# Moving GpSimd's two-input elementwise operations to VectorE's queue in a two-layer decoder trunk

## The chip, the core and the metric

The kernel runs on one core of one Trainium2 chip. The metric is the device time of one execution in microseconds (us); the time before is the median of three runs. Below, PE is TensorE's matmul pipe, DVE is VectorE, ACT is ScalarE, POOL is GpSimd and SP is SyncE, whose queue issues every DMA of this kernel.

## The reference, cut to what matters

The input x is 512 tokens by 1024 features, in float32, and there are two layers. For each layer six modulation vectors come from one matrix product of silu(c) with ada_w.

```
h    = x * (1 + scale1) + shift1
proj = h @ w_in                      # 512 columns a, 512 u, 512 v
y_a  = trailing-window means of a (windows 2, 4, 8, 16) minus a, times pool_w, times pool_scale
y_b  = gelu(u) * (tril(W_s) @ layernorm(gelu(v)) + b), per head, in chunks of 128 tokens
x    = layernorm(alpha * x + gate1 * (concat(y_a, y_b) @ w_out))
h    = x * (1 + scale2) + shift2
g, val = split(h @ w_up)
x    = layernorm(alpha * x + gate2 * ((gelu(causal_conv3(g)) * val) @ w_down))
```

## The kernel before, in words

Each engine takes its instructions in the order in which the program writes them. PE computes every large product in three passes over float32r parts: weights and activations are each split into a high part (a rounded copy) and a low part (the value minus the high part), and the passes are high by high, high by low and low by high.

**Weights.** SP loads 512 KB blocks of 128 x 1024 into one of seven buffers `raw`. `wsplit_next` (L116) makes the high part `whi` on ACT (L132) and then the low part `wlo` with one two-input subtraction (L135). `refill(n, eng, defer)` (L153) does this for the next n weights and orders loads ahead; `eng` says which engine takes the subtraction, VectorE if nothing is given. A `raw` buffer is free again when its subtraction has been done, and the load that takes the buffer waits for that in SP's queue.

**Modulation sums.** `ada_sum` (L180) is one DVE operation of 128 x 1024 over a loaded `raw` block with an accumulated column. `first_h` (L458) runs two of them for each of the eight k-tiles of the first layer's h, and `pump` (L229) spreads the others between other work. These blocks share the seven `raw` buffers with the weights.

**Start.** For each k-tile SP loads two ada_w blocks, a tile of x and zero to two w_in blocks; `first_h` forms the scale and shift columns, the high part `hh` (DVE, L466), the exact value (ACT, L467) and the low part `hl` (L468, on DVE for the first two k-tiles and on POOL for the other six). PE takes each k-tile as it comes.

**Token mixing.** `window_sums(g, eng)` (L535) doubles windows by shifted adds (L540) and small copies (L541); `pool_group` (L547) finishes a group. `v_norm` (L571) normalizes v; `z_mix` (L584) and `pool_mix` (L558) make the eight inputs of the output projection and free their PSUM banks. In layer 0 all this stands between PE's u tiles, its z and pm products and the output projection (`project`, L340, with the products in L336 to L338).

**Norms.** `project_and_norm` (L353) computes the second half of a projection chunk by chunk (four chunks of 128 tokens), with `residual` (L287: a multiplication out of PSUM, L291, and an add into `xr`, L292), statistics, `rstd_of` (two tiny POOL operations, L274 and L275), the normalization (L383), transposes (L298) and `modulate` (L301), whose low part `hl` is L313. While the last chunk is under way up to three weights are prepared; the subtraction of the first stands before that chunk's residual, those of the others behind its statistics:

```
refill(4 - len(ready), G, lows)
...
mv, rs = rstd_of(sts[c], f"{tag}{c}")
for f in lows[1:]:
    f()
```

`next_residuals` (L316) runs eight POOL operations of 128 x 1024 behind a norm (L318, L319). `norm_rows` loads the rows g and b that they need, behind the weights in SP's queue, and ACT scales them (L327). `project_and_end` (L389) is the last norm.

Before the change POOL's queue takes these two-input operations, besides `next_residuals` and the tiny ones: the low parts of the first layer's w_in and w_out and of the weights prepared in a norm's last chunk, six of the eight `hl` of the start, the windows of pooling group 3 in layer 0, the adds of three first-half residuals in each of the three inner norms, and four such adds in the last one.

Of the kernel before, what the change touches and what calls it, by code (L numbers as in the profile page):

```python
# [38 lines left out]
def trunk(ctx: ExitStack, tc: tile.TileContext, a: dict, out: bass.AP):  # L39
# [10 lines left out]

    # each engine takes its instructions in the order they are written here
    ctx.enter_context(tc.manual_schedule())
# [14 lines left out]

    # ---- constants; 2 silu(c) along every partition
    c_in = const.tile([P, KD], F32, name="c_in")
# [25 lines left out]

    # ---- the weights in the order of their use: float32 in, two float32r parts out
    order = []
# [55 lines left out]
    def refill(n=1, eng=None, defer=None, in_units=False):  # L153
        """Prepares the next n weights, as far as there is room for them."""
        for _ in range(n):
            if count["split"] < len(order) and (in_units or count["live"] < N_SPLIT):
                wsplit_next(in_units, eng, defer)
                while count["load"] < min(len(order), count["split"] + count["ahead"]):
                    wload()
# [8 lines left out]
    def mm3(ps, w, x, start, stop):  # L168
        """ps += (wh + wl).T @ (xh + xl)"""
        T.matmul(ps, w[0], x[0], start=start, stop=False)  # L170
        T.matmul(ps, w[0], x[1], start=False, stop=False)  # L171
        T.matmul(ps, w[1], x[0], start=False, stop=stop)  # L172

    # ---- adaLN: columns of silu(c) @ ada_w, 128 at a step, that fill in between other work
    ada = [(0, v) for v in (2, 4, 3, 5)] + [(1, v) for v in (1, 0, 2, 4, 3, 5)]
# [17 lines left out]
    def gate_start(l, v):  # L193
        """The gate's columns on the diagonals of blocks, in two float32r parts."""
        g = modc[l][:, 8 * v : 8 * v + 8]
        gh = small.tile([P, KD], F32R, tag="gh", name=f"gh{l}_{v}")
        gl = small.tile([P, KD], F32R, tag="gl", name=f"gl{l}_{v}")
        V.tensor_copy(gh, g)
        V.tensor_tensor(gl, g, gh.bitcast(F32), op=ALU.subtract)
        out_ = []  # L200
        for hf in range(2):
            for part in (gh, gl):
                d = unit(f"gd{l}_{v}_{hf}", F32R)
                V.tensor_tensor(
                    d.rearrange("p (j n) -> p j n", j=4),
                    ident.unsqueeze(1).to_broadcast([P, 4, P]),
                    part[:, 4 * hf : 4 * hf + 4].bitcast(F32).unsqueeze(2).to_broadcast([P, 4, P]),
                    op=ALU.mult,
                )
                out_.append(d)  # L210
        return out_

    def ada_flush(now=False):
        """Gates along every partition: the diagonals two calls after the columns, the products
        two calls later."""
        for due in ada_due:
            due[0] += 1
            if due[3] is None and (now or due[0] >= 2):
                due[3] = gate_start(*due[1:3])
        while ada_due and (now or ada_due[0][0] >= 4):  # L220
            _, l, v, d = ada_due.pop(0)
            gates[l, v] = rows.tile([P, D], F32, tag="gate", name=f"gate{l}_{v}")
            for hf in range(2):
                ps = bank(f"gate{l}_{v}_{hf}")
                T.matmul(ps, ones_r, d[2 * hf], start=True, stop=False)
                T.matmul(ps, ones_r, d[2 * hf + 1], start=False, stop=True)
                A.copy(gates[l, v][:, halves(hf)], ps)

    def pump(n=1, upto=None):  # L229
        """n steps of the sums, as far as these are for the vectors upto."""  # L230
        for _ in range(n):
            i = ada_at["step"]
            if i >= len(ada) or (upto is not None and ada[i][:2] not in upto):
                return
            ada_load(max(0, min(i + 1 + ADA_AHEAD, len(ada)) - ada_at["load"]))
            l, v, n_ = ada[i]
            ada_sum(l, v, n_, ada_raw.pop(0))
            if n_ == KD - 1:
                o = slice(8 * v, 8 * v + 8)
                V.tensor_tensor(modc[l][:, o], modc[l][:, o], cols[l][:, C_ADAB + 8 * v : C_ADAB + 8 * v + 8], op=ALU.add)  # L240
                if v in (2, 5):
                    ada_due.append([0, l, v, None])
            ada_at["step"] += 1

    def weave(gens, side=()):
        """The steps of gens in turn, those of side in between."""
        gens, side = list(gens), list(side)
        while gens or side:
            gens = [g for g in gens if next(g, 0) is None]
            if side:  # L250
                side.pop(0)()

    def affine_cols(l, sub, g, b):
        """Columns A, B with h = n * A + B, from the last norm's g and b and the modulation."""
        o = 24 * sub
# [12 lines left out]

    # ---- post-norm: xr holds the sum; leaves n, h, and the next residual
    def rstd_of(st, name):  # L270
# [7 lines left out]
    def affine_norm(t, mv, rs, g, b, pieces=1, after=None):  # L278
        """t = (t - mean) * rstd * g + b"""
        V.scalar_tensor_tensor(t, t, mv[:, 0:1], g, op0=ALU.subtract, op1=ALU.mult)  # L280
# [6 lines left out]
    def residual(ps, c, hf, gate, eng=None, f=slice(0, HALF)):  # L287
        """Columns f of half hf."""
        t = unit(f"res{c}_{hf}")
# [4 lines left out]
    def turn(c, tag):  # L294
        """n of one chunk, transposed."""
        ps = [bank(f"tr_{tag}{c}_{hf}") for hf in range(2)]
# [4 lines left out]
    def modulate(c, ps, tag, AB):  # L301
        """h of one chunk from its transposed n, in two halves."""
        ca, cb = AB
# [26 lines left out]
    def pair_mms(ps, c, w, act, i, n, f=slice(0, HALF)):  # L330
        """A pair of k-tiles i, i + 1 of n, for columns f of one chunk."""
        cs = slice(c * P, (c + 1) * P)
# [7 lines left out]
    def project(act, hf, name, after):  # L340
        """All chunks at once against streamed weights; after(i) follows each pair."""
        ps = [bank(f"{name}{hf}_{c}") for c in range(NCH)]
# [10 lines left out]
    def project_and_norm(act, ps0, gate, tag, AB):  # L353
        """The second half chunk by chunk, each chunk's norm under the next one's products.
        ps0 holds the first half. Leaves the last chunk to be turned."""
        n = len(act)
# [4 lines left out]
        for c in range(NCH):  # L361
# [6 lines left out]
            if c == NCH - 1:  # L368
                refill(4 - len(ready), G, lows)
                for f in lows[:1]:  # L370
                    f()
# [14 lines left out]
            if c + 1 < NCH:  # L386
                residual(ps0[c + 1], c + 1, 0, gate, G)

    def project_and_end(act, ps0, gate, grow, brow):  # L389
        """The same at the end, where the norm goes out; the last chunk's columns in two parts."""  # L390
        n = len(act)
# [6 lines left out]
        def first_half(c):  # L398
            sts[c] = small.tile([P, 4, 6], F32, tag="st4", name=f"end{c}")
            residual(ps0[c], c, 0, gate, G)  # L400

# [30 lines left out]
    def after_norm(name, tag, AB):  # L432
        """The first four tiles after a norm: in halves of the tokens, the last chunk turned
        in the midst of the first half."""
        tiles = []
# [11 lines left out]

    # ---- start: modulation of the first layer and h from x, one k-tile after the other
    A0 = const.tile([P, KD], F32, name="A0_0")
# [8 lines left out]
    def first_h(k, x, raw):  # L458
# [8 lines left out]
        A.activation(x, x, AF.Identity, bias=B0[:, o], scale=A0[:, o])  # L467
        (V if k < 2 else G).tensor_tensor(hl[:, k, :], x, hh[:, k, :].bitcast(F32), op=ALU.subtract)  # L468

    def v_mms(ps, w, k):  # L470
        """k-tile k of all chunks of v, tokens on partitions."""
        wh, wl = w[0](4 * (k % 2), 4)
# [8 lines left out]
    for k in range(KD):  # L481
        at = first_load(k)
        new = FIRST[k]
        wload(len(new))
        refill(min(1, len(new)), G)
        first_h(k, *at)
        refill(len(new) - 1, G)
        fresh = []
# [16 lines left out]
    wload(3)  # L505
    refill(1, G)
    count["ahead"] = AHEAD
    done = [ps for ps, w in tiles]

    for l in range(L):  # L510
        col = cols[l]

        # ======== token mixing
        fill = () if l else ((0, 2), (0, 4), (0, 3))
# [95 lines left out]

        lo_eng = None if l else G
        if l:
# [10 lines left out]
        else:  # L623
            pump(PRE_FILL, fill)
            refill(1, G)
        w3 = wst.rearrange("p (h t) -> p h t", h=4)
# [11 lines left out]
        for i in range(4):  # L638
# [10 lines left out]
            if i == 0 and l == 0:  # L649
                window_sums(2, V)  # L650
                window_sums(3, G)
                pool_group(2)
# [22 lines left out]

        # ======== channel mixing
        more = l + 1 < L
# [122 lines left out]
```

## Time and profile before

| | |
|---|---|
| runs, us | 1043.29, 1040.75, 1042.89; median 1042.89 |
| profiled execution | span 1041.6 us, from its first to its last instruction; no other time of it is given |
| PE busy | 990.9 us (95%) |
| DVE busy | 695.7 us (67%) |
| ACT busy | 352.8 us (34%) |
| POOL busy | 214.0 us (21%), 136 instructions |
| mean granted TensorE clock | 0.980 |

The span is the time from the first to the last instruction of one profiled execution; it lies inside the range of the three runs, 1.3 us under their median. A busy share is an average over the whole span, and the stages of this kernel differ.

### The profile page before, as it was taken

The page shows a single profiled execution, that of the slowest core. Times are in us where ns is not written, and L with a number is a line of the kernel's source. Part 1 is how long each engine was busy: PE and PEld are TensorE (multiplying, and loading weights), DVE is VectorE, ACT ScalarE, POOL GpSimd, SP SyncE. Part 2 cuts the span into 40 slices and gives each one's busy share as a digit, 9 for nine tenths or more (in the row PEclk, how much of TensorE's full clock was granted, in tenths as well). Part 3 has the DMA queues.
Part 4 walks back from the last instruction along what each step waited for, and adds up shares of the span by engine and source line. Part 5 has one row for each costly group of instructions (what it writes and reads, how often), then busy time and mean ns, then how long its engine had stood idle before and what let it go on. Part 6 is the DMA issues. An engine that isn't in the chain of part 4 may idle for free.

```text
span 1041.6 us, 11987 instructions
## 1 busy us (share of the span) xinstructions
PE 990.9 (95%) x4654; PEld 826.8 (79%) x4654; DVE 695.7 (67%) x896; ACT 352.8 (34%) x495; POOL 214.0 (21%) x136
## 2 busy tenths in 40 slices
PE   5996889999999999999999999999999999999996
PEld 4785568888888888888888878888888888888886
DVE  6989998788673456757579973878744245444446
ACT  3242316443432123334254331644343212333210
POOL 4647245800000000000039300680000000000022
PEclk7998899999999999999999999999999999999999
DMA  9873772276574336547603422227433332334002
GB/s 334 306 276 110 287 279 76 90 259 211 194 228 135 102 101 200 183 147 257 203 21 114 160 81 81 83 94 250 141 101 101 101 101 81 101 101 142 21 1 81
DMA packets 44695, 154.57 MB, mean 148 GB/s; under 512 B 5216, under 2 KB 5472, under 8 KB 44640
## 3 DMA queue, kind: packets, MB, share of 16 engines
q1 hardware_dynamic: 44640, 153.82, 43.6%
q8 instruction: 36, 0.59, 0.2%
q14 instruction: 19, 0.16, 0.0%
HBM read 151.71 MB, written 2.10 MB: 148 GB/s over the span
## 4 chain that ended last, share of the span: by engine, by line
PE 82%; DVE 10%; POOL 3%; DMA 2%; issue 2%; ACT 1%; SPq 0%; DVEq 0%; POOLq 0%; ACTq 0%
PE up L171 15%; PE up L172 15%; PE up L170 15%; PE down L336 6%; PE down L338 6%; PE down L337 6%; PE n_pj L336 2%; PE n_pj L338 2%; PE n_pj L337 2%; DVE raw_ada L182 2%; POOL wlo L135 1%; DMA b<-in_ln_b_dram 1%; PE out L338 1%; PE v L475 1%; PE v L476 1%
## 5 line engine op out<-in xcount | busy, mean ns | idle before, releaser
L171 PE MATMUL up<-hl,whi 128*128 128x512 f32 (+1 forms) x768 | 285.6, 372 | 4.8 <-DVE hl L313 4.8
L172 PE MATMUL up<-hh,wlo 128*128 128x512 f32 (+1 forms) x768 | 285.4, 372 | 1.0 <-POOL wlo L135 1.0
L170 PE MATMUL up<-hh,whi 128*128 128x512 f32 (+1 forms) x768 | 285.5, 372 | 0.0
L135 DVE TENSOR_TENSOR wlo<-raw_w_up,whi 128x1024 fp32r<-128x1024 f32 x81 | 111.7, 1381 | 135.6 <-ACT whi L132 135.6
L171 PEld LDWEIGHTS up<-hl,whi 128*128 128x128 f32 x768 | 144.6, 188 | 30.5 <-DVE hl L313 5.6
L172 PEld LDWEIGHTS up<-hh,wlo 128*128 128x128 f32 x768 | 144.6, 188 | 26.4 <-POOL wlo L135 1.4
L170 PEld LDWEIGHTS up<-hh,whi 128*128 128x128 f32 x768 | 144.6, 188 | 24.9
L135 DVE TENSOR_TENSOR wlo<-raw_w_down,whi 128x1024 fp32r<-128x1024 f32 x44 | 53.9, 1225 | 114.0 <-ACT whi L132 114.0
L132 ACT CAST whi<-raw_w_up 128x1024 fp32r<-128x1024 f32 x88 | 91.0, 1045 | 69.1 <-PE down L338 52.6
L182 DVE SCALAR_TENSOR_TENSOR raw_ada<-raw_ada,c 128x1024 f32<-128x1024 f32 x80 | 106.4, 1341 | 4.1 <-DMA raw_ada<-in_ada_w_dram 4.1
L336 PE MATMUL down<-whi,gh 128*128 128x512 f32 x272 | 105.8, 389 | 0.0
L337 PE MATMUL down<-wlo,gh 128*128 128x512 f32 x272 | 105.8, 389 | 0.0
L338 PE MATMUL down<-whi,gl 128*128 128x512 f32 x272 | 105.8, 389 | 0.0
L274 POOL TENSOR_SCALAR rs_n<-mv_n 128x1 f32<-128x1 f32 x12 | 5.8, 485 | 397.5 <-DVE mv_n L272 397.5
L292 POOL TENSOR_TENSOR xr<-res,xr 128x512 f32<-128x512 f32 x13 | 16.6, 1289 | 321.8 <-DVE res L291 319.6
L694 ACT ACTIVATE y<-y 128x512 f32<-128x512 f32 x44 | 27.9, 634 | 148.8 <-DVE y L691 148.8
L132 ACT CAST whi<-raw_w_down 128x1024 fp32r<-128x1024 f32 x44 | 46.0, 1047 | 74.8 <-PE down L338 74.8
L684 ACT ACTIVATE y<-up,cols 128x512 f32<-128x512 f32 x44 | 34.3, 779 | 80.0 <-PE up L172 80.0
L338 PEld LDWEIGHTS down<-whi,gl 128*128 128x128 f32 x272 | 51.1, 188 | 10.6
L336 PEld LDWEIGHTS down<-whi,gh 128*128 128x128 f32 x272 | 51.1, 188 | 10.6
L337 PEld LDWEIGHTS down<-wlo,gh 128*128 128x128 f32 x272 | 51.1, 188 | 10.6
L310 ACT ACTIVATE ht_n<-tr_n,B,A 128x128 f32<-128x128 f32 x96 | 36.1, 455 | 57.2 <-PE tr_n L298 41.2
(155 smaller groups left out, 1620.7 us busy)
## 6 DMA issues: line engine op xcount, KB each, us to landing
raw_w_up<-in_w_up_dram SPq DMA_DIRECT2D x88, 512.0 KB, 3.3
raw_ada<-in_ada_w_dram SPq DMA_DIRECT2D x80, 512.0 KB, 4.2
raw_w_down<-in_w_down_dram SPq DMA_DIRECT2D x44, 512.0 KB, 3.3
raw_w_in<-in_w_in_dram SPq DMA_DIRECT2D x24, 512.0 KB, 4.3
raw_first<-in_ada_w_dram SPq DMA_DIRECT2D x16, 512.0 KB, 5.3
raw_w_out<-in_w_out_dram SPq DMA_DIRECT2D x16, 512.0 KB, 4.1
xT<-in_xT_dram SPq DMA_DIRECT2D x8, 256.0 KB, 5.4
xr<-in_x_dram SPq DMA_DIRECT2D x4, 512.0 KB, 6.5
```

The lines of the kernel that those rows point to most:

```text
L132: A.copy(hi, src)
L135: (eng or V).tensor_tensor(lo, src, hi.bitcast(F32), op=ALU.subtract)
L170: T.matmul(ps, w[0], x[0], start=start, stop=False)
L171: T.matmul(ps, w[0], x[1], start=False, stop=False)
L172: T.matmul(ps, w[1], x[0], start=False, stop=stop)
L182: V.scalar_tensor_tensor(raw, raw, 0.5, c2, op0=ALU.mult, op1=ALU.mult, accum_out=modc[l][:, o : o + 1])
L310: A.activation(tmp[:, w], ps[hf][:, w], AF.Identity, bias=cb[:, k : k + 1], scale=ca[:, k : k + 1])
L336: T.matmul(ps[:, f], ah[:, cs], wh, start=i + j == 0, stop=False)
L337: T.matmul(ps[:, f], ah[:, cs], wl, start=False, stop=False)
L338: T.matmul(ps[:, f], al[:, cs], wh, start=False, stop=i + j == n - 1)
L684: A.activation(y, pg, AF.Identity, bias=col[:, C_CB + j : C_CB + j + 1], scale=col[:, cw + 2 : cw + 3])
L694: A.activation(y, y, AF.Gelu_apprx_tanh)
```

## The change

Every `tensor_tensor` of POOL up to the norms' end goes to VectorE's queue, at the place in the program where it stood: `refill` is no longer given GpSimd, the first layer's `hl` are all on VectorE, so are the four windows of group 3 with their four small copies, and the first-half residual adds. `next_residuals`, `rstd_of` and the mask of the spatial weights stay on POOL. The other lines of the diff take comments away.

```diff
-                refill(4 - len(ready), G, lows)
+                refill(4 - len(ready), None, lows)
...
-                residual(ps0[c + 1], c + 1, 0, gate, G)
+                residual(ps0[c + 1], c + 1, 0, gate)
...
-            residual(ps0[c], c, 0, gate, G)
+            residual(ps0[c], c, 0, gate)
...
-        (V if k < 2 else G).tensor_tensor(hl[:, k, :], x, hh[:, k, :].bitcast(F32), op=ALU.subtract)
+        V.tensor_tensor(hl[:, k, :], x, hh[:, k, :].bitcast(F32), op=ALU.subtract)
...
-        refill(min(1, len(new)), G)
+        refill(min(1, len(new)))
         first_h(k, *at)
-        refill(len(new) - 1, G)
+        refill(len(new) - 1)
...
-    refill(1, G)
+    refill(1)
...
-        lo_eng = None if l else G
+        lo_eng = None
...
-            refill(1, G)
+            refill(1)
...
-                window_sums(3, G)
+                window_sums(3, V)
```

## Rows read from the trace of the kernel before

**Rows 1.** Busy time by stretch: length, engines' busy us, PE clock, DMA share, GB/s.

```profile
84.00:115.20 31.20, 17.85 (x67) 11.71 (x65) 30.75 (x50) 3.96 (x7) 15.17 (x11) 0.80 0.44 164
115.20:150.70 35.50, 35.50 (x146) 28.81 (x146) 34.38 (x45) 12.54 (x16) 15.89 (x5) 0.94 0.76 270
150.70:190.50 39.80, 30.87 (x191) 27.57 (x190) 30.79 (x37) 23.27 (x47) 24.16 (x18) 0.91 0.27 94
190.50:547.00 356.50, 356.50 (x1642) 297.97 (x1643) 232.62 (x318) 122.63 (x166) 24.59 (x17) 1.00 0.51 168
```

**Rows 2.** PE's waits over the whole span: us in total, times, longest.

```profile
PE pm L560 <- DVE z L586: 4.4, 1, 4.4
...
PE a L171 <- POOL hl L468: 2.0, 2, 1.8
```

**Rows 3.** PE in order of time, where the first inner norm's transposes begin.

```profile
155.61 1.97 PE L298 MATMUL tr_n<-ident,xr 128*128 128x128 f32 x8 [4.91 <-DVE xr L383]
```

**Rows 4.** POOL's groups by form over the span: busy us, mean ns, idle before.

```profile
L135 POOL TENSOR_TENSOR wlo<-raw_w_in,whi 128x1024 fp32r<-128x1024 f32 x14 | 38.5, 2757 | 20.6 <-ACT whi L132 20.6
...
L135 POOL TENSOR_TENSOR wlo<-raw_w_out,whi 128x1024 fp32r<-128x1024 f32 x8 | 23.2, 2919 | 25.4 <-ACT whi L132 25.4
L135 POOL TENSOR_TENSOR wlo<-raw_w_up,whi 128x1024 fp32r<-128x1024 f32 x7 | 19.0, 2733 | 1.5 <-ACT whi L132 1.5
L292 POOL TENSOR_TENSOR xr<-res,xr 128x512 f32<-128x512 f32 x13 | 16.6, 1289 | 321.8 <-DVE res L291 319.6 <-PE n_pj L338 2.2
```

**Rows 5.** DVE's groups by form from 300 to 500 us.

```profile
L182 DVE SCALAR_TENSOR_TENSOR raw_ada<-raw_ada,c 128x1024 f32<-128x1024 f32 x25 | 30.4, 1218 | 0.0
L135 DVE TENSOR_TENSOR wlo<-raw_w_up,whi 128x1024 fp32r<-128x1024 f32 x20 | 24.5, 1225 | 39.1 <-ACT whi L132 39.1
```

**Rows 6.** DVE in order of time, start: start us, us, instruction, idle before.

```profile
11.50 2.19 DVE L468 TENSOR_TENSOR hl<-xT,hh 128x512 fp32r<-128x512 f32 x1 [0.88 <-ACT xT L467]
...
31.21 2.35 DVE L462 SCALAR_TENSOR_TENSOR A<-modc,cols 128x1 f32<-128x1 f32 x1
33.48 0.15 DVE L465 TENSOR_TENSOR B<-modc,cols 128x1 f32<-128x1 f32 x1
33.66 2.51 DVE L466 TENSOR_SCALAR hh<-xT,A,B 128x512 fp32r<-128x512 f32 x1
```

**Rows 7.** POOL in order of time, at the start and in the second inner norm.

```profile
30.15 5.74 POOL L135 TENSOR_TENSOR wlo<-raw_w_in,whi 128x1024 fp32r<-128x1024 f32 x2
...
552.27 2.86 POOL L318 TENSOR_TENSOR xr<-xr,g 128x1024 f32<-128x1024 f32 x1
```

**Rows 8.** DVE in order of time, layer 0's token mixing up to its norm.

```profile
78.39 2.96 DVE L280 SCALAR_TENSOR_TENSOR v<-v,mv_v,sg 128x512 f32<-128x512 f32 x1
...
110.86 1.28 DVE L586 TENSOR_TENSOR z<-z,sb 128x512 f32<-128x512 f32 x2
...
139.84 3.42 DVE L182 SCALAR_TENSOR_TENSOR raw_ada<-raw_ada,c 128x1024 f32<-128x1024 f32 x1
...
149.49 0.68 DVE L291 TENSOR_TENSOR res<-out,gate 128x512 f32<-128x512 f32 x1
```

**Rows 9.** DVE in order of time: group 3's windows in layer 1, and what follows.

```profile
588.44 0.68 DVE L540 TENSOR_TENSOR ws<-at 128x511 f32<-128x511 f32 x1
...
591.63 0.69 DVE L550 SCALAR_TENSOR_TENSOR pooled<-ws,at 128x512 f32<-128x512 f32 x1
```

**Rows 10.** The chain that ended last, in the first and the third inner norm.

```profile
175.90 6.42 DMA b<-in_ln_b_dram
...
185.49 4.93 DVE hl L313 x2
...
670.35 5.77 DMA b<-in_ln_b_dram
```

**Rows 11.** DVE in order of time, last chunk of the second inner norm.

```profile
547.24 2.85 DVE L383 TENSOR_SCALAR xr<-xr,mv_n,rs_n 128x1024 f32<-128x1024 f32 x1 [0.77 <-POOL rs_n L275]
```

**Rows 12.** POOL's waits over the whole span: us in total, times, longest.

```profile
POOL wlo L135 <- ACT whi L132: 47.5, 9, 15.2
```

## Prediction

> **What bounds the kernel now.** I read the page first: PE is 95% busy, so only PE's idle and slow stretches can be won. The busy times by stretch [rows 1] say where they lie. From 190.5 to 547 us PE is busy all the time at full clock, and time saved elsewhere passes through such a stretch unchanged. From 84 to 115.2 us PE works 17.85 of 31.2 us and DVE 30.75; from 115.2 to 150.7 us both are full; in the first norm, up to 190.5 us, PE works 30.87 of 39.8. PE's waits [rows 2] name DVE or POOL as what ended them, and the transposes of the first norm [rows 3] come after 4.91 us of waiting for DVE's normalization. So before 190 us DVE's queue sets the end.
>
> The second reading is why DVE is full. With POOL idle a modulation sum takes 1.22 us and a weight's low part 1.23 [rows 5]. In order of time the same forms take 2.2 us more as soon as POOL is at work: a sum takes 3.42 [rows 8], an operation on one single element takes 2.35 us where its neighbour of the same size takes 0.15 [rows 6]. That one ends at 33.56, within POOL's pair of low parts that runs from 30.15 [rows 7]: the DVE operation stands until a POOL operation is through, however little it does itself.
>
> **What the change moves, part by part.** On POOL 29 low parts go: 14 of 2.76 us, 8 of 2.92, 7 of 2.73; and 13 adds of 1.29 us [rows 4], six `hl` of the start and group 3's windows with them. On DVE a low part costs 1.23 us [rows 5]; group 3's windows, copies included, cost 3.19 us, from 588.44 to 591.63, where POOL is quiet [rows 9]. No DMA is moved, but each load that waits for a `raw` buffer now waits in DVE's order.
>
> *Start, to 38.5 us.* Between 11.50 and 33.66 DVE has seven operations stretched by POOL, 13.2 us over their clean times together (the first and the last in [rows 6]). They go. DVE gets six low parts (7.4 us) and one `hl` (0.6). The first low part now stands in front of the first sums and waits for its block to land and be cast: about 3.2 us of new idle time, and some 1 us for casts later. Net 13.2 - 7.4 - 0.6 - 4.2 = 1.0 earlier at the fourth k-tile, where PE waits 1.8 us for POOL's `hl` [rows 2]. From there to 84 us PE never waits. I take -1.0 us; bounds +3 (if the late first step is not made good) and -1.8 (the whole wait).
>
> *Token mixing, 71 to 149.5 us.* Here DVE has 14 stretched operations, from 78.39 to 139.84 (the first and the last in [rows 8]), 24.9 us over their clean times: 14.0 us before z at 110.86, 10.9 after. DVE gets ten low parts and group 3's windows, 10 x 1.23 + 3.19 = 15.5 us: five low parts and the windows, 9.3 us, before z. So z comes 14.0 - 9.3 = 4.7 us earlier. That matters to PE, since the fourth pm product waits 4.4 us for the bank that z frees [rows 2] and the output projection begins behind it. The sums end 24.9 - 15.5 = 9.4 us earlier, and the residual at 149.49 [rows 8] with them. PE's own work between the two points is unbroken (35.50 of 35.50 us, [rows 1]), so PE reaches the transposes 4.7 us earlier, 4.9 us before which it stood idle for DVE anyway [rows 3]: 4.7 + 4.9 = 9.6, about DVE's 9.4. Both arrive together; I take -9.4. Bounds: 0 if the gain of DVE is eaten by waits for DMA and casts, -10.5 if group 3's windows overlap better.
>
> *First norm, 155 to 190.5 us.* Three things. With PE no longer idle for 4.9 us, the first eight transposes don't take 1.97 us, and the mean clock of this stretch is 0.91 [rows 1, 3]; 39.8 us at 0.09 less is 3.6 us at most, of which I take 2. Then the rows g and b: SP issues them behind a weight load that waits for POOL's low part; b's load begins at 175.90 [rows 10], lands at 182.3 and ACT, in order, scales it before it can modulate the last chunk; the DVE low parts behind it end at 190.4. With the low part on DVE ahead of the last residual the buffer is free some 2.5 us earlier relative to the products, and b stops being last by about 2. Against that, two low parts (2.46 us) stand in DVE's queue before the last normalization, which is no longer stretched by 2.0: +0.4. Each first-half add moved is 0.7 us more on DVE per chunk, hidden where the add out of `xr` was stretched by POOL's 1.29 us [rows 4]. Sum -2 - 2 + 0.4 = -3.6; bounds 0 and -6.
>
> *Second norm, about 547 us.* Here g and b are there already, and what holds `next_residuals` back is POOL's own low parts: it begins at 552.27 [rows 7], after the last normalization began at 547.24 [rows 11]. Without them POOL begins as soon as its last tiny operation is done, which is when the normalization could begin [rows 11], or sooner than DVE gets to it with two more low parts ahead; then it alternates with DVE on the second low part, `hl`, the normalization and `hl` again. Two POOL operations of about 2.4 us in front of the normalization, against one now (547.24 takes 2.85), and 1.2 us for the low part: I take +3; bounds 0 and +6.
>
> *Third norm, about 670 us.* The same chain through b as in the first [rows 10], without the idle PE before it: -2.5; bounds 0 and -3. *The last norm*: four adds of 0.7 us come while PE has a product of a whole chunk under way; nothing, and if that cover were gone 4 x 0.7 = 2.8. *Elsewhere* nothing moves, and PE is full.
>
> The sum: -1.0 - 9.4 - 3.6 + 3.0 - 2.5 = -13.5. The profiled span of 1041.6 becomes 1028.1; the runs' median stands 1.3 above the span, so the forecast is 1029.4.
>
> **A rule that speaks against it.** DVE is busy for 30.75 of 31.2 us where this work is added [rows 1], and 24.9 us of its stretched rows come while POOL works [rows 8]. The Trainium skill (Perfetto Trace Analysis, Optimizing Scalar/DVE Operations) says that taking work off a saturated DVE, even to GpSimd, may make sense, but that between these two engines it might not help, because they share an SBUF read port. By its first half the move back should cost, about as in the rival of the fuller DVE below, 1063; by its second half the sum above stands, and so far the stretched rows agree with the second.
>
> **Rivals.**
>
> *Loads become the bound.* DVE would take 0.52 MB in 1.23 us, 427 GB/s. From 115.2 to 150.7 us the DMA engines moved 270 GB/s at a share of 0.76 [rows 1], so a full share gives about 355 GB/s, 1.48 us for each block. For the 15 blocks from the end of token mixing on this is 15 x 0.25 = 3.7 us, if the seven buffers don't hide it. Then the time is about 1033. For it: DVE will have nearly no slack. Against: the loads of the whole stretch, some 21 x 1.48 = 31 us, just fit in it.
>
> *Norm tails.* `next_residuals` begins earlier in all three norms, not in the second alone, and the low parts on DVE fall into it. Then the first and third lose their 2 to 2.5 us of gain and pay 3 each: about 1029.4 + 4.5 + 6 = 1040, no change. Against: there POOL must wait for g, which DMA brings late [rows 10].
>
> *A full DVE only gets fuller* (slower). If the stretched rows were not POOL's doing, the clean times would not come back: +15.5 us up to the residual, +8.0 at the start, of which PE hides some 3, and nothing won: about 1042.9 + 20 = 1063. It decides if DVE's sums keep taking 3.4 us with POOL idle; 25 sums at 1.22 us with POOL idle [rows 5] speak against it.
>
> *Casts hold up DVE's queue* (slower). POOL waited 47.5 us for casts [rows 12]; on POOL only its own queue stood behind that, on DVE the sums and residuals do. It turns the sign once more than 13.5 + 3 = 16.5 of these 47.5 us come back as DVE idle on the path; with half of them, 23.8, the time is about 1042.9 - 13.5 + 23.8 = 1053. Against: POOL waited because it had nothing else to do; DVE, full as it is [rows 1], arrives at a low part later than POOL did and mostly finds the cast done.
>
> **How the numbers follow.** A measurement of this kernel tells about 0.3%, 3.1 us, from no change. I give the forecast 0.60 (1024 to 1033), the loads 0.18 (1031 to 1037), the tails 0.10 (1036 to 1042), the fuller DVE 0.03, the casts 0.05, and 0.04 to a larger gain, where the bounds of the norms and of token mixing fall together (1018 to 1024). Faster: 0.60 + 0.18 + 0.04 and half of the tails, 0.87; the same 0.05; slower 0.08. The range is 1021 to 1040, which leaves out the two slower cases and the ends of the others.
>
> **What would show it.** No DVE operation of 128 x 1024 over 1.3 us between 71 and 150 us, except beside `next_residuals`; DVE's z near 105 and its first residual near 139; the transposes of the first norm near 145 with a wait under 1.5 us; g and b issued right behind the first low part of the last chunk; in the second norm the normalization some 3 us later, relative to the products before it, with `next_residuals` already under way. The prediction is wrong if DVE shows idle time of several us for casts or loads between 75 and 140, or if the stretched durations stay.

## The result, and the profile after

The changed kernel takes 1030.41 us (median of 4 runs, 1029.47 to 1030.85) against 1042.88 for the kernel before beside it, a ratio of 0.9887 with a 95% interval of 0.9871 to 0.9902. The forecast was 1029.4. The profiled span fell from 1041.6 to 1028.6 us.

The page's first part gives each engine's busy time and its instructions in the changed kernel:

```profile
PE 987.2 (96%) x4654; PEld 826.1 (80%) x4654; DVE 676.2 (66%) x952; ACT 352.7 (34%) x495; POOL 103.5 (10%) x80
```

DVE took on 56 operations, and its busy time fell by 19.5 us. What it lost is the time in which it stood for POOL. The busy times of the two stretches of token mixing (columns as in [rows 1]):

```profile
84.00:115.20 31.20, 19.95 (x70) 13.27 (x70) 30.82 (x61) 6.52 (x10) 0.00 (x0) 0.73 0.68 238
115.20:150.70 35.50, 35.50 (x163) 29.43 (x162) 32.79 (x57) 14.16 (x22) 1.91 (x4) 1.00 0.69 250
```

DVE is as full as before in the first stretch [rows 1], but does 61 operations there instead of 50. In order of time it shows what became of [rows 8]:

```profile
105.33 1.28 DVE L586 TENSOR_TENSOR z<-z,sb 128x512 f32<-128x512 f32 x2
106.53 1.22 DVE L182 SCALAR_TENSOR_TENSOR raw_ada<-raw_ada,c 128x1024 f32<-128x1024 f32 x1
...
136.61 1.22 DVE L182 SCALAR_TENSOR_TENSOR raw_ada<-raw_ada,c 128x1024 f32<-128x1024 f32 x1 [0.20 <-DMA raw_ada<-in_ada_w_dram]
...
138.53 0.69 DVE L291 TENSOR_TENSOR res<-out,gate 128x512 f32<-128x512 f32 x1
```

z comes at 105.33 (forecast: near 105) and the first residual at 138.53 (near 139). A sum takes 1.22 us where one took 3.42, and the only wait for a load in this stretch is 0.20 us. PE's waits over the span (us in total, times, longest):

```profile
PE v L475 <- DVE hh L466: 8.2, 1, 8.2
PE tr_n L298 <- DVE xr L383: 7.4, 4, 2.5
PE pm L560 <- ACT u L645: 6.3, 1, 6.3
PE pm L560 <- DVE z L586: 4.2, 1, 4.2
PE a L171 <- DVE hl L468: 3.0, 3, 1.1
```

The 4.91 us ahead of the first norm's transposes [rows 3] are gone; the longest of the four waits for the normalization is now 2.5 us. Two waits stand out. The one at the start grew from 4.0 to 8.2 us. The other, 6.3 us for ACT in token mixing, is new. In order of time, ACT:

```profile
98.18 1.04 ACT L132 CAST whi<-raw_w_out 128x1024 fp32r<-128x1024 f32 x1 [18.71 <-DMA raw_w_out<-in_w_out_dram]
99.13 0.59 ACT L645 ACTIVATE u<-u 128x512 f32<-128x512 f32 x1
```

ACT stands for a weight that lands at 98.2 us, with the gelu of u behind the cast, and PE's next product waits for the bank that this gelu frees. Before, ACT stood 14.8 us for the same load and PE came later than it. It doesn't set the end here: DVE is busy for 30.82 of the 31.20 us, and PE waits for its z right after. Following PE's starts of the same products in both profiles gives the change term by term; the offset at the end of each stretch less the one at its beginning:

| stretch, and PE's starts at its end | forecast | measured |
|---|---|---|
| start, fourth k-tile 38.48 to 37.02 | -1.0 | -1.5 |
| token mixing, first transposes 155.61 to 144.78 | -9.4 | -9.4 |
| first norm, offset then -13.6 | -3.6 | -2.8 |
| second norm, offset then -12.0 | +3.0 | +1.7 |
| third norm, offset then -13.1 | -2.5 | -1.1 |
| sum | -13.5 | -13.1 |

### The profile page after: what moved, and what is told of

It is laid out like the page before. It is cut to its first block, busy times and chain, and to the rows that moved or that the text cites. A ratio compares the mean times of both kernels' runs of the same rounds, so it can differ in the third digit from the quotient of the medians.

```text
span 1028.6 us, 11962 instructions
## 1 busy us (share of the span) xinstructions
PE 987.2 (96%) x4654; PEld 826.1 (80%) x4654; DVE 676.2 (66%) x952; ACT 352.7 (34%) x495; POOL 103.5 (10%) x80
## 4 chain that ended last, share of the span: by engine, by line
PE 78%; DVE 14%; DMA 3%; issue 2%; POOL 1%; ACT 1%; SPq 1%; DVEq 0%; POOLq 0%; ACTq 0%
PE up L171 15%; PE up L170 15%; PE up L172 15%; PE down L338 6%; PE down L337 6%; PE down L336 6%; DVE wlo L135 2%; DMA raw_ada<-in_ada_w_dram 2%; DVE raw_ada L182 1%; DVE raw_first L182 1%; DVE res L291 1%; DVE stn L377 1%; DVE xr L292 1%; DVE xr L383 1%; PE n_pj L338 1%
## 5 line engine op out<-in xcount | busy, mean ns | idle before, releaser
L135 DVE TENSOR_TENSOR wlo<-raw_w_up,whi 128x1024 fp32r<-128x1024 f32 x88 | 118.1, 1346 | 139.4 <-ACT whi L132 139.4
L182 DVE SCALAR_TENSOR_TENSOR raw_ada<-raw_ada,c 128x1024 f32<-128x1024 f32 x80 | 97.0, 1219 | 2.4 <-DMA raw_ada<-in_ada_w_dram 2.1
L135 DVE TENSOR_TENSOR wlo<-raw_w_in,whi 128x1024 fp32r<-128x1024 f32 x24 | 37.6, 1591 | 11.7 <-ACT whi L132 11.7
```

The costliest lines, as they stand in the source:

```text
L135: (eng or V).tensor_tensor(lo, src, hi.bitcast(F32), op=ALU.subtract)
L182: V.scalar_tensor_tensor(raw, raw, 0.5, c2, op0=ALU.mult, op1=ALU.mult, accum_out=modc[l][:, o : o + 1])
```

## Experiments

**Each part alone.** Three kernels start from the kernel before and take over one part of the change. The first, token mixing:

```diff
     wload(3)
-    refill(1, G)
+    refill(1)
...
-        lo_eng = None if l else G
+        lo_eng = None
...
             pump(PRE_FILL, fill)
-            refill(1, G)
+            refill(1)
...
-                window_sums(3, G)
+                window_sums(3, V)
```

> Of the change only the token mixing of layer 0 (its low parts and group 3's windows) goes to VectorE; the start and the norms keep their GpSimd operations. Port theory (what the change gives back is VectorE time that GpSimd's operations had stretched, nearly all of it here): the first residual comes 9 to 11 us earlier, 149.49 to about 139.5, the first norm's transposes lose their 4.9 us of waiting, and the whole is 10 to 12 us faster, about 1031.5. Rival (GpSimd's slower low parts held up PE and the loads, each moved one paying alike): 11 of 29 low parts are moved, so some 11/29 of 12.5 us, 4.7 faster, about 1038.

Measured: 1032.36 us, ratio 0.9904 (0.9887 to 0.9921). The first residual comes 10.4 us earlier, PE's first transposes 10.4, PE's products behind the first norm 11.5, and nothing changes from there to the end. This part is most of the gain. The rival's 1038 is out.

The second, the start:

```diff
-        refill(min(1, len(new)), G)
+        refill(min(1, len(new)))
         first_h(k, *at)
-        refill(len(new) - 1, G)
+        refill(len(new) - 1)
...
-    (V if k < 2 else G).tensor_tensor(hl[:, k, :], ...)
+    V.tensor_tensor(hl[:, k, :], ...)
```

> Of the change only the start goes to VectorE: eight low parts and six hl. Port theory: PE is 1.5 us earlier from the fourth k-tile to 84 us, but z after it waits for VectorE, whose sums from 60 us on wait for their loads and whose stretched operations are all still there: 0 to 1.5 us faster at the end, 1041.4 to 1042.9. Rival (each moved low part pays alike): 8/29 of 12.5, 3.4 us faster, about 1039.5.

Measured: 1042.74 us, ratio 0.9994 (0.9983 to 1.0006): no change that can be told, between 1.8 us faster and 0.6 slower. The rival's 1039.5 is out. PE's first wait for `hh` is 9.7 us here and 8.2 in the changed kernel, though both have the same instructions up to there; DVE's first low part waits 8.50 us for its cast in the one and 7.27 in the other. A term of 1 us at the start can't be told from such scatter.

The third, the norms:

```diff
-                refill(4 - len(ready), G, lows)
+                refill(4 - len(ready), None, lows)
...
-                residual(ps0[c + 1], c + 1, 0, gate, G)
+                residual(ps0[c + 1], c + 1, 0, gate)
...
-            residual(ps0[c], c, 0, gate, G)
+            residual(ps0[c], c, 0, gate)
```

> Of the change only the norms go to VectorE: ten low parts and 13 adds. Port theory: the first norm 1 to 2 us faster because the rows g and b are no longer issued behind GpSimd's low part, the second 1.7 us slower because the next residuals begin before the last normalization, the third 1 us faster: 0 to 2 us faster, about 1042. Rival (each moved low part pays alike): 10/29 of 12.5, 4.3 us faster, about 1038.5.

Measured: 1039.08 us, ratio 0.9963 (0.995 to 0.9975), some 3.9 us, more than the theory's 0 to 2. In the profile 1.4 us of the span's 5.3 are there at the first residual, ahead of every edited instruction; the first norm gives 3.1, the second costs 0.3, the third gives 1.1. The places are those of the forecast and the theory's sum was too small. The number alone is that of the rival (1038.5), by which each moved low part pays alike; the first two parts speak against that. The three parts alone make 17.1 us in the spans (11.5, 0.3, 5.3, with the 1.4 of scatter), together 13.0: what the parts win is not independent.

**Is it the taking of turns?** Four kernels keep the change and add work to POOL beside DVE in the first layer's token mixing. The first lets POOL compute each of the stretch's low parts a second time, into a tile that nobody reads:

```diff
                 (eng or V).tensor_tensor(lo, src, hi.bitcast(F32), op=ALU.subtract)
+                if twin:
+                    G.tensor_tensor(twin[0], src, hi.bitcast(F32), op=ALU.subtract)
```

> The changed kernel, but in layer 0's token mixing GpSimd computes each low part a second time, into a spare buffer that nothing reads; VectorE's own work and the values are those of the changed kernel. Port theory: GpSimd's 11 operations stretch VectorE's two-input operations again by about 2.2 us each, some 20 to 24 us up to the first residual, on top of the moved work: 1048 to 1055. Rival (GpSimd's own slowness was the cost, on what waits for its results): nothing that PE or VectorE needs comes from GpSimd here; only the raw buffers come free later, 0 to 5 us: 1030 to 1036.

Measured: 1053.11 us, ratio 1.0096 (1.0082 to 1.011). DVE's queue is that of the changed kernel, and the first residual comes at 162.9 instead of 138.5. But this POOL operation also keeps a weight's buffer from being freed. The next three take that away: ACT writes one column of the spare tile for each low part, and POOL then works on that tile alone, in three ways.

```diff
+                if twin:
+                    A.activation(twin[0][:, 0:1], hi[:, 0:1].bitcast(F32), AF.Copy)
+                    G.tensor_tensor(twin[0], twin[0], twin[0], op=ALU.subtract)     # two reads
+                    for _ in range(3): G.tensor_copy(twin[0], twin[0])              # or: one read
+                    for _ in range(3): G.memset(twin[0], 0.0)                       # or: no read
```

> As with the fills, but one subtraction of the spare tile from itself for each low part: two SBUF operands, and nothing that another engine or a load waits for (work that is added). It parts the two things that the recomputed low parts mixed, which also kept a weight's buffer from being freed. Theory (it is the taking of turns): 12 operations of about 2.8 us each cost DVE what they take beside it, sums above 1.5 us, the first residual 15 to 25 us later, 1044 to 1054. Rival (most of the 24 us came from buffers freed late): sums stretched on the spot but the residual less than 8 us later, 1030 to 1038.

> As with the fills beside the first layer's token mixing, but each fill is a copy of the spare tile onto itself: POOL reads one operand from SBUF and writes it, three times 128 x 1024 for each low part (work that is added). Theory (POOL stands in DVE's way as soon as it reads SBUF at all, which the rule on the two sides in the Trainium skill, SBUF — State Buffer, SBUF: two separate sides, would give): sums stretched above 1.5 us, the first residual more than 8 us behind the changed kernel's 138.5, time 1040 to 1065. Rival (only a POOL operation with two SBUF operands locks DVE out): sums at 1.22 us, the residual within 2 us of 138.5, time 1028 to 1034.

> The changed kernel, with POOL at work beside DVE through the first layer's token mixing again, but with operations that only write: for each low part of that stretch ACT copies one column and POOL then fills a spare tile three times with zeros (128 x 1024 each, work that is added). It asks whether any POOL operation stands in DVE's way, or one that reads SBUF. Theory (the two engines exclude each other by what both read; the rule of the Trainium skill that a DVE operation with two SBUF inputs only blocks against a GpSimd operation that reads SBUF, SBUF — State Buffer, SBUF: two separate sides, would give this too): DVE's sums stay near 1.22 us, the first residual stays within 2 us of 138.5, and the time is 1030 to 1033. Rival (any POOL operation on SBUF takes its turn with DVE): sums above 1.5 us, the first residual more than 10 us later, 1042 to 1058, as with the recomputed low parts (1053).

Measured: 1047.51 us, ratio 1.0043 (1.0028 to 1.0058), for two reads; 1055.44, 1.0116 (1.0098 to 1.0135), for one read; 1029.35, 0.9868 (0.9846 to 0.989), for none. Groups by form from 70 to 165 us (busy us, mean ns, idle before), first with two reads, then one, then none:

```profile
L138 POOL TENSOR_TENSOR twin<-twin 128x1024 f32<-128x1024 f32 x11 | 25.0, 2276 | 45.9 <-ACT twin L137 45.9
...
L185 DVE SCALAR_TENSOR_TENSOR raw_ada<-raw_ada,c 128x1024 f32<-128x1024 f32 x19 | 29.8, 1595 | 0.0
```

```profile
L139 POOL COPY twin<-twin 128x1024 f32<-128x1024 f32 x34 | 53.1, 1561 | 31.6 <-ACT twin L137 30.2
...
L186 DVE SCALAR_TENSOR_TENSOR raw_ada<-raw_ada,c 128x1024 f32<-128x1024 f32 x18 | 28.9, 1632 | 0.0
```

```profile
L139 POOL MEMSET twin<- 128x1024 f32 x33 | 31.5, 954 | 28.2 <-ACT twin L137 26.9
...
L186 DVE SCALAR_TENSOR_TENSOR raw_ada<-raw_ada,c 128x1024 f32<-128x1024 f32 x18 | 21.5, 1222 | 0.2 <-DMA raw_ada<-in_ada_w_dram 0.2
```

With fills POOL is busy for 31.5 us beside DVE, and DVE's sums stay at 1222 ns; with 25.0 us of subtractions they take 1595, with copies 1632. The first residual comes at 138.6, 157.5 and 164.3 us. So 25.0 us of subtractions cost 19.0 us without a buffer freed late, where the 33.7 us of recomputed low parts cost 24.4: about three quarters of POOL's busy time in both. What counts is not that POOL works, but that it reads SBUF beside DVE's operations. The Trainium skill (SBUF — State Buffer, Who interferes with whom) states that a DVE instruction with two SBUF inputs contends with a GpSimd instruction that reads SBUF, not with one that only writes it; these three rows agree. DVE and POOL in order of time, in the kernel with two reads, show the turns themselves: an operation on v that takes 0.74 us with POOL idle stands until POOL's 1.99 us are through.

```profile
84.16 1.99 POOL L138 TENSOR_TENSOR twin<-twin 128x1024 f32<-128x1024 f32 x1 [0.31 <-ACT twin L137]
...
84.32 2.38 DVE L283 SCALAR_TENSOR_TENSOR v<-v,mv_v,sg 128x512 f32<-128x512 f32 x1
...
88.92 0.74 DVE L283 SCALAR_TENSOR_TENSOR v<-v,mv_v,sg 128x512 f32<-128x512 f32 x1
```

**The norms' tails.** The changed kernel's second norm, DVE, POOL and PE in order of time:

```profile
531.11 2.31 DVE L135 TENSOR_TENSOR wlo<-raw_w_in,whi 128x1024 fp32r<-128x1024 f32 x2
...
533.94 2.85 DVE L383 TENSOR_SCALAR xr<-xr,mv_n,rs_n 128x1024 f32<-128x1024 f32 x1
...
532.45 1.40 POOL L275 TENSOR_TENSOR rs_n<-rs_n,neg_half 128x1 f32<-128x1 f32 x1
533.82 2.42 POOL L318 TENSOR_TENSOR xr<-xr,g 128x1024 f32<-128x1024 f32 x1
...
536.84 1.94 PE L298 MATMUL tr_n<-ident,xr 128*128 128x128 f32 x8 [2.20 <-DVE xr L383]
```

One operation of `next_residuals` starts 0.12 us ahead of the normalization, which then takes 2.85 us, as before [rows 11]. Two edits go at this. The first makes POOL begin with the last chunk, for which it must wait:

```diff
     def next_residuals(grow, brow):
-        for c in range(NCH):
+        for c in reversed(range(NCH)):
```

> The changed kernel, with the order of the chunks in next_residuals turned round: the last chunk comes first, so POOL has to wait for that chunk's transposes and stands still while DVE normalizes it. Theory (what the second norm lost, 1.65 us, is POOL's first operation at 533.82 in front of the last normalization, and the lower clock behind PE's longer wait): the normalization behind the second norm's last residual takes under 1 us instead of 2.85, PE's wait there falls from 2.2 to under 1 us, the second norm gives back 1.5 to 3 us, the first and third 0 to 1 each: 1026 to 1029. Rival (the wait there is set by the chain residual, statistics, rstd on ACT and POOL, not by next_residuals): PE's wait stays above 1.8 us and the time at 1030 to 1031. Second rival: the first chunks' residuals come too late for the products behind them: 1031 to 1036.

Measured: 1024.93 us, ratio 0.9825 (0.9804 to 0.9846). In order of time, the second norm of this kernel:

```profile
533.25 0.81 DVE L383 TENSOR_SCALAR xr<-xr,mv_n,rs_n 128x1024 f32<-128x1024 f32 x1
...
535.35 2.41 POOL L318 TENSOR_TENSOR xr<-xr,g 128x1024 f32<-128x1024 f32 x1 [2.18 <-PE tr_n L298]
...
534.12 1.09 PE L298 MATMUL tr_n<-ident,xr 128*128 128x128 f32 x8 [0.15 <-DVE xr L383]
```

The normalization takes 0.81 us and PE waits 0.15. The second norm gives back 3.6 us and the third 1.5, somewhat more than the theory's 3 and 1. In the second norm it was right in the cause: 2.0 us are the wait, the rest is the granted clock, which stays at 1.00 from 530 to 540 us here and is 0.85 in the changed kernel. The third norm's 1.5 is not the theory's: PE's wait there stays as it was (2.48 and 2.46 us), since POOL had not come ahead of that normalization, and what changed is the clock behind it (1.00 from 660 to 670 us, 0.83 in the changed kernel). Some 0.7 us more of this profile's gain is there before any norm, scatter.

The second edit puts the last chunk's low parts, all but the first, behind the normalization:

```diff
-            for f in lows[1:]:
-                f()
...
             V.tensor_scalar(xr[c], xr[c], mv[:, 0:1], rs, ...)
+            for f in lows[1:]:
+                f()
```

> The changed kernel, with the second low part of each norm's last chunk moved from ahead of that chunk's normalization to behind it in DVE's queue. Theory (DVE's queue order prices the last normalization, so that what stands ahead of it costs PE its full time): the normalization comes 1.2 to 2.3 us earlier in the second and third norm and up to 1 us earlier in the first, PE's waits of 2.2 to 2.5 us for it fall by as much, 1026 to 1029. Rival (the low part is done while the rstd chain on ACT and POOL runs anyway, so DVE would wait for that instead): the normalization starts at the same time, 1030 to 1031; and where the low part behind it delays the last hl or a weight, up to 1033.

Measured: 1036.16 us, ratio 0.9925 (0.9901 to 0.9949), some 4 us worse than the change by the ratios. The theory was right on the wait and wrong on the sum. PE's waits for the last normalizations fell as it had it, from 2.2 to 2.5 us to between 0.8 and 1.1. But in this kernel's second norm the two low parts behind the normalization run beside `next_residuals`, and PE waits for those:

```profile
534.46 6.71 DVE L135 TENSOR_TENSOR wlo<-raw_w_in,whi 128x1024 fp32r<-128x1024 f32 x2
...
537.88 0.38 PE L172 MATMUL in<-hh,wlo 128*128 128x256 f32 x1 [1.96 <-DVE wlo L135]
```

In the changed kernel the same two take 2.31 us and fall into the time in which POOL works out the rstd. That takes POOL 2.49 us beside them and 1.12 here without them: they were not hidden there, but cost 1.4 us instead of more.

**The start.** In the changed kernel each step of the start that prepares a weight begins with a low part; this edit puts it behind the step's sums, `hh` and ACT's x, so ahead of `hl`:

```diff
-        refill(min(1, len(new)))
-        first_h(k, *at)
+        lows = []
+        refill(min(1, len(new)), None, lows)
+        first_h(k, *at, lows)
...
         A.activation(x, x, AF.Identity, bias=B0[:, o], scale=A0[:, o])
+        for f in lows:
+            f()
```

> The changed kernel, with the first low part of each step of the start behind that step's sums, hh and x instead of ahead of them in DVE's queue. Theory (the start's term: the low part in front of the first sums holds DVE for its cast, and PE's first wait of 8.2 us, against 4.0 before, comes from it): the first product comes 2 to 3 us earlier, the fourth k-tile 0 to 3 us earlier, but behind it the sums at 60 us wait for their loads (2.1 us by the changed kernel's rows), so the end gains 0 to 2 us: 1028.5 to 1030.5. Rival (the weights' low parts are what the products of the start need soonest): the first products wait for the low part instead, fourth k-tile the same or up to 2 us later, 1030 to 1033.

Measured: 1020.13 us, ratio 0.9776 (0.9759 to 0.9794), far beyond the 0 to 2 us expected. DVE in order of time, the changed kernel:

```profile
10.50 1.23 DVE L135 TENSOR_TENSOR wlo<-raw_w_in,whi 128x1024 fp32r<-128x1024 f32 x1 [7.27 <-ACT whi L132]
11.64 1.22 DVE L182 SCALAR_TENSOR_TENSOR raw_first<-raw_first,c 128x1024 f32<-128x1024 f32 x1
...
15.68 0.69 DVE L468 TENSOR_TENSOR hl<-xT,hh 128x512 fp32r<-128x512 f32 x1 [0.88 <-ACT xT L467]
```

and with the sums first:

```profile
7.45 1.23 DVE L182 SCALAR_TENSOR_TENSOR raw_first<-raw_first,c 128x1024 f32<-128x1024 f32 x1 [4.08 <-ACT c L86]
...
11.73 1.23 DVE L135 TENSOR_TENSOR wlo<-raw_w_in,whi 128x1024 fp32r<-128x1024 f32 x1 [1.13 <-ACT whi L132]
12.88 0.69 DVE L470 TENSOR_TENSOR hl<-xT,hh 128x512 fp32r<-128x512 f32 x1
```

Two things are won: DVE starts its sums at 7.45 instead of 11.64, and the low part fills the 0.88 us that DVE otherwise waits for ACT's x in each of eight steps (7.1 us in all, then 1.8). The fourth k-tile comes 6.4 us earlier on PE; by the second norm it is 7.2 us, and 9.7 behind the third, since the clock does not fall in these two. The expectation held that the sums at 60 us would wait for their loads; they wait 0.7 us here, 1.9 in the changed kernel. Loads are issued when DVE frees their buffers, and from 20 to 40 us they moved 404 GB/s here, 326 there. The limit was DVE's order, not the DMA engines.

**A kernel that beats both.** The start in this order and the residuals reversed, together; then with the last low parts behind the normalization as well:

> The changed kernel with two of the edits together: the start's first low parts behind the sums (alone 1020.1) and next_residuals from the last chunk on (alone 1024.9). Theory (the two act in different stretches, and the second norm's part of the sums-first gain, a granted clock that did not fall, is the only thing both win): the product of the two ratios, 0.9776 x 0.9825 / 0.987 for what the changed kernel has already, would be 1015; less up to 1.5 for the shared part: 1014 to 1017. Rival (an earlier start makes the residuals' later finish the bound): 1018 to 1021.

> The first kernel of this call (sums first, residuals reversed) with the second low part of each norm's last chunk behind the normalization as well, which alone cost 6 us. Theory (alone it cost because next_residuals ran on POOL beside the low part and the hl behind it: 6.71 us for two low parts and 8.41 for three hl in the second norm; with POOL standing still until the transposes, that falls away): 1 to 2 us better than the first kernel of this call in the norms. Rival (PE needs that low part before it needs the transposes, whatever POOL does: it waited 2.0 us for it): 1 to 5 us worse than the first kernel of this call.

Measured: 1016.99 us (1016.27 to 1018.45), ratio 0.975 (0.9731 to 0.9769), for the two; 1017.7 (1017.51 to 1018.03), 0.9757 (0.9739 to 0.9774), for all three. Against the changed kernel the profiled span is 9.7 us shorter with the sums first, 5.8 with the residuals reversed and 12.0 with both. So the two add, less 3.6 us: the 1.3 us of the second norm's clock is won by each alone, and in the third norm, where each alone won 1.2 to 1.5 us, the clock fell again in the kernel with both (0.75 from 648 to 653 us). The third edit makes no difference that can be told: what it cost alone is gone now that POOL stands still there, but neither its theory's gain nor its rival's loss shows. On PE in the first norm it brings the last transposes 1.4 us earlier, relative to the products before them, and behind the norm 0.5 of it is left.

## Why the prediction was right, point by point

*Token mixing, -9.4.* Right in size, place and cause. z, the residual and the transposes came within half a microsecond of where the forecast put them, this part alone gave 10.4 us there, and POOL operations that read SBUF brought the stretched rows back, while fills did not. The rival of a fuller DVE, and with it the first half of the Trainium skill's sentence (Perfetto Trace Analysis, Optimizing Scalar/DVE Operations), is out here: DVE stayed full and the kernel got faster with the work on it. Its second half, that moving work from one of these two engines to the other might not help, agrees: with these operations on POOL the kernel was 12.5 us slower.

*The rivals.* Loads held DVE for 0.20 us in token mixing, casts for 0.26; 16.5 us would have been needed to turn the sign. The one long wait for a load is ACT's. The rival of the norms' tails fell by the reason given against it: in the first and third norm POOL waits for g (1.65 and 0.48 us) and begins behind the last normalization.

*Start, -1.0.* Measured -1.5, but alone nothing that can be told: the term is as large as the scatter of the first load. The step in it, that the first low part makes DVE wait for its cast, was right and, in this execution, of the size that I gave it: DVE's first sum began before at

```profile
7.46 1.23 DVE L182 SCALAR_TENSOR_TENSOR raw_first<-raw_first,c 128x1024 f32<-128x1024 f32 x1 [4.15 <-ACT c L86]
```

and the low part now stands in its place after 7.27 us of waiting, 3.1 more. The sum left out that each `hl` that moves makes DVE wait 0.88 us for ACT's x: eight times now, twice before. I took 3.2 us of new idle time as the price of the move; the sums-first kernel shows that it was the price of the order in which the move was made, and the start had some 6.5 us to give on PE.

*First norm, -3.6.* Measured -2.8, and in part by luck. The first term was right: PE no longer stands still ahead of the transposes, the granted clock of 0.50 from 155 to 160 us is gone, and this gives 2.4 us, with token mixing alone too; I had 2. In the rest of the norm I had 1.6 more, and 0.4 came. SP issues b at 161.67 instead of 175.90, 14.2 us earlier, but the products beside it come 13.3 earlier, so b gains 0.9 us on them and not 2.5. PE's wait for the last normalization grew by 1.2 us, from 1.28 to 2.49, and not by 0.4; and behind it the clock fell. PE in order of time, before:

```profile
179.26 1.09 PE L298 MATMUL tr_n<-ident,xr 128*128 128x128 f32 x8 [1.28 <-DVE xr L383]
...
187.66 0.39 PE L171 MATMUL up<-hl,whi 128*128 128x256 f32 x1 [1.45 <-DVE hl L313]
...
190.47 0.39 PE L171 MATMUL up<-hl,whi 128*128 128x256 f32 x1 [1.11 <-DVE hl L313]
```

and after, with the window behind it (columns as in [rows 1]; the clock before was 1.00 there):

```profile
167.17 1.09 PE L298 MATMUL tr_n<-ident,xr 128*128 128x128 f32 x8 [2.49 <-DVE xr L383]
```

```profile
169.00:174.00 5.00, 5.00 (x34) 5.00 (x33) 2.15 (x2) 4.94 (x12) 4.92 (x3) 0.73 0.22 89
```

PE comes to the two products that waited for `hl` 2.7 us later in the norm, 1.2 by the wait and 1.5 by the clock, and waits for neither. So b left the chain [rows 10] in good part because PE was late. With the norms alone changed, where the clock stayed at 1.00 there, the rest of the norm gives 2.4 us.

*Second norm, +3.0.* The step that failed is "two POOL operations of about 2.4 us in front of the normalization". One came, as before; the normalization begins 0.3 us later relative to the products and not 3, and PE's wait grew by 0.34 us, from 1.86 to 2.20. With the norms alone changed that 0.3 is all that the second norm loses. In the changed kernel 1.3 more goes behind the wait, where the eight transposes take 1.94 us instead of 1.09: the granted clock from 534 to 539 us is 0.79 and from 539 to 544 0.87, where it was 1.00 before. The windows of the changed kernel (columns as in [rows 1]):

```profile
534.00:539.00 5.00, 2.80 (x16) 2.60 (x15) 5.00 (x3) 1.03 (x3) 4.92 (x3) 0.79 0.53 179
539.00:544.00 5.00, 5.00 (x38) 5.00 (x38) 4.38 (x3) 4.94 (x10) 4.92 (x2) 0.87 0.01 3
```

*Third norm, -2.5.* b left the chain here too. PE's waits fell from 4.3 us (1.3 for the normalization, 2.2 for `hl`, 0.8 for a low part) to one of 2.5, which is -1.8; the rest of the measured -1.1 answers again to the clock, 0.72 from 661 to 666 us. So in all three norms the fall of the clock behind the last wait was left out.

The sum was right to 0.4 us in part because errors of opposite sign (0.8 and 1.4 of gain too much, 0.5 too little, 1.3 of loss too much) cancel. The other 0.6 us between 1029.4 and 1030.4 is the median's distance from the profiled span, 1.3 us before and 1.8 after.

## What to carry to other kernels

When rows of DVE have a clean duration and a long one, look at what POOL reads in the meantime: an operation that costs POOL's idle time is not free if it reads SBUF beside a full DVE; fills were. When work comes to a full in-order queue, its place decides as much as its length: put it into a wait that the queue has anyway (here for ACT's x), not ahead of what the next engine is standing for. The two edits that follow from this gave as much again (1030.4 to 1017.0 us) as the change itself.

## What was unexpected in the hardware

The turns go both ways, and down to the smallest operation: in the second norm POOL's operation on 128 x 1 takes 1.40 us beside DVE's low parts, and 0.57 in the kernel with the low parts behind the normalization, where DVE has none at that time.

Fills did not leave DVE quite alone. In order of time, in the kernel with fills, a copy of 128 x 4 and a cast of 128 x 8, which take 0.16 and 0.17 us in the changed kernel, take 0.50 and 0.94 beside them:

```profile
88.60 0.50 DVE L547 COPY ws<-ws 128x4 f32<-128x4 f32 x1
...
100.71 0.94 DVE L202 CAST gh<-modc 128x8 fp32r<-128x8 f32 x1
```

Both read one operand. Two other copies took 0.28 us, the rest 0.14 to 0.17; operations with two operands in SBUF kept their clean times beside the fills. What parts the copies, no run here shows.

The granted clock fell behind PE's wait of 2.20 us in the second norm of the changed kernel, and not behind the same wait of 2.20 us with the norms alone changed (1.00 from 543 to 553 us) or with the sums first, in this window of that kernel:

```profile
527.00:532.00 5.00, 2.80 (x25) 2.60 (x24) 5.00 (x2) 1.64 (x5) 4.92 (x3) 1.00 0.43 152
```

PE's busy time is the same 2.80 of 5.00 us in the windows of all three; 0.79 is a mean over time at 2.4 and at 1.2 GHz. Why it fell in the one and not in the other stays open; each profile shows one execution, and no run here tells it apart.
